# When a kernel loads its weight blocks, and when it begins to sum them: one transformer trunk on one NeuronCore

## The chip, the core and the metric

The kernel runs on one core of a Trainium2 chip, as one program. The metric is the device time of that program in microseconds (us); the median of the runs counts. The core has a matrix engine (TensorE, PE in the profile, with its weight loads as PEld), a vector engine (VectorE, DVE), a scalar engine (ScalarE, ACT), GpSimd (POOL) and SyncE (SP). SP and POOL issue the DMA transfers that this text is about; all transfers of the core run on the same 16 DMA engines.

## The reference

One residual stream of 512 tokens by 1024 features passes a short gated convolution layer, a feed-forward layer, a sliding-window attention layer with sinks, and a second feed-forward layer, each with a norm before and after it. The change touches the two feed-forward layers:

```python
D_MODEL = 1024; SEQ = 512; DEPTH = 2; D_FF = 2816
def swiglu(h, w_gate_up, w_down):
    g, u = jnp.split(h @ w_gate_up, 2, axis=-1)
    return (jax.nn.silu(g) * u) @ w_down
...
    ff = swiglu(rmsnorm(h, ffn_pre_norm[l]), ffn_w_gate_up[l], ffn_w_down[l])
    h = h + rmsnorm(ff, ffn_post_norm[l])
```

All data are float32. The kernel keeps that precision by splitting every operand into a high and a low part of a reduced float type and adding three matmuls for each product (high times low, high times high, low times high).

## The kernel before

**Products of 2x2 blocks.** Most large matrix products are done by blocks with seven products instead of eight (P1 to P7). For that, some products need weight blocks that are sums of others. The kernel makes these sums in DRAM while it runs: POOL issues DMAs that copy a block of 512 KB into a tile `hsum` and DMAs that add another block onto it. A copy is one kind of transfer here, an accumulate the other.

**Stages of a feed-forward layer.** The 22 feature tiles are taken as follows. Two go first, without the block scheme (`project_first`). The other 20 make ten pairs, called q0 to q9 here; each is a list of seven jobs, P1, P2, P6, P5, P7, P3, P4 (`gate_jobs`). Between them stand four lists of jobs for the down projection, d0 to d3 (`down_jobs`): d0 has 11 jobs, the others seven. The order is q0 q1 q2 d0 q3 q4 d1 q5 q6 d2 q7 q8 q9 d3. The last four weight blocks of the layer stand among q9 and d3 as jobs of their own.

**The line of jobs.** `in_line` (L474) walks through these jobs. Weight blocks arrive in seven buffers of 512 KB (`N_RAW = 7`, pool `wraw`), loaded by SP at L440, tile `raw`. For job j, `prepare(j)` splits its block: ACT writes the high part `whi` (L469), DVE the low part `wlo` (L470). This runs three jobs ahead of TensorE (`LINE_LEAD = 3`). After that DVE's read, the buffer is free, and `prepare` lets further loads be written into the program. A load waits on SP for the release of the buffer it takes. DVE adds two blocks in place (L457) where a product's sum is not made in DRAM: in pairs with a number in `ADDED` (1, 2, 3, 4, 5 and 7) only two sums are made in DRAM, `ab` and `ac`. There, block a11 is read by jobs P1, P6 and P3, and a12 by P2 and P3, so these two buffers are held longer than the ones loaded after them.

**The sums' plan.** `BEGIN` (L29) names, for each point of the program, the sum whose making begins there: `g07` is layer 0, pair q7; `d02` is layer 0, down list d2. Points: `0f0` and `0f1` lie in and behind `project_first` of layer 0, `0p3` at the end of q3, `0s1` at the end of d1. At each point `sum_on` (L558) first issues what is left, then gives the next step of each sum that is under way. A sum begins with its copies (two, or four where four tensors are made), goes on with two accumulates, and where four tensors are made, with one more and one more: two or four steps, one a point. The DMAs of a step go to a list, and behind each job `issue` (L529) takes `1 + len(issues) // 6` of them, each held back until ACT has made the high part of the block of job j + 3, so that they are paced.

The rule for loads, as it stands, is this one line (L488): the load with number n may be written when the block loaded seven before it has had its last use.

Of the kernel before, what the change touches and what calls it, by code (L numbers as in the profile page):

```python
# [27 lines left out]

BEGIN = {  # L29
# [4 lines left out]
}  # L34


# [18 lines left out]
N_SLOT, N_WIDE, N_RAW, N_W = 43, 14, 7, 4  # L55
# [17 lines left out]
def yoco_kernel(  # L73
# [400 lines left out]
    def in_line(jobs, late, paced=True):  # L474

        raws = []
        for j, job in enumerate(jobs):
            for raw in job.raws:
                if raw not in raws:
                    raws.append(raw)  # L480
                raw.last = j
        n = [0]

        def prepare(j):

            if 0 <= j < len(jobs):
                jobs[j].prepare()
            while n[0] < len(raws) and (n[0] < N_RAW or raws[n[0] - N_RAW].last <= j):  # L488
                raws[n[0]].fetch()
                n[0] += 1  # L490
            if j + 1 < len(jobs):
                jobs[j + 1].add()

        for j in range(-1, LINE_LEAD):
            prepare(j)
        late = late()
        for j, job in enumerate(jobs):
            if job.run:
                job.run(job)
            prepare(j + LINE_LEAD)  # L500
            if paced and j + LINE_LEAD < len(jobs):
                issue(1 + len(issues) // 6, jobs[j + LINE_LEAD].begun)
            for _ in range(1 if paced else max(len(late) - 1, 1)):
                if late and not job.alone:
                    late.pop(0)()
            late += job.then() or [] if job.then else []
# [22 lines left out]
    def issue(n, behind=None):  # L529

        for dst, src, op in issues[:n]:
            if len(dst.shape) == 3:
                dst, src = (t.rearrange("k (a b) c -> (k a) (b c)", b=4) for t in (dst, src))
            else:
                dst, src = (t.rearrange("(a b) c -> a (b c)", b=2) for t in (dst, src))
            kw = {} if op is None else {"accum_op": op}
            made = tc.keep_in_program_order(
                nc.gpsimd.dma_start(dst, src, max_dma_last_dim=4 * 4 * S, **kw))  # L538
            if behind is not None:
                tc.add_manual_dep(  # L540
                    made.ins, behind.ins.name, mybir.DependencyInfo(
                        mybir.DependencyClass.Sync, mybir.DependencyReason.DATA),
                    reason="pace")
        del issues[:n]
# [115 lines left out]
    with tc.manual_schedule(engines=ALL):  # L660
# [25 lines left out]
        for k in range(KT):  # L686
# [7 lines left out]
            for i in range(3):  # L694
                for t in range(3):
                    n = 3 * k + t
# [117 lines left out]
    with tc.manual_schedule(engines=ALL):  # L814
        project(begun[1][2], ws[2], xs)

        def late():
            parts = []
            for f in range(2):
                first, second, taps, third, end = conv(f)  # L820
                first(begun[f][0])
                second(begun[f][1])
                parts += [taps, lambda third=third, f=f: third(begun[f][2])]
                sum_on(f"c{f}")
                issue(len(issues))
            return parts + end()
# [645 lines left out]
    with tc.manual_schedule(engines=ALL):  # L1472
        sum_on("a0")
        for i in range(KT + 2):
# [6 lines left out]
            for c in ORDER.split():  # L1481
# [9 lines left out]
                op, n = c[0], [int(d) for d in c[1:].rstrip("-")]  # L1491
                t = i - late
                if op == "g":

                    u = 2 * (t - EARLY - 1) + n[0]
                    if u in (-2, -1, 2, 3):
                        j = u + 2 if u < 0 else u
# [8 lines left out]
                elif op == "G":  # L1506
                    t += LEAD + 1
                    of = qs
                    if KT <= t < KT + 4:
                        j = t - KT  # L1510
# [107 lines left out]
```

## Time and profile before

| | |
|---|---|
| median of 3 runs | 1024.08 us (1023.93 to 1025.08) |
| the profiled execution, its own time | 1026.6 us |
| span in that profile, first to last instruction | 1024.8 us |
| TensorE clock granted in it | 0.998 of full speed |
| TensorE busy | 1013.6 us, 99% |
| DVE, ACT, POOL busy | 857.8, 580.7, 196.7 us |
| feed-forward layer 0, q0 to the first job of d3 | 204.25 to 472.04 us |
| feed-forward layer 1, the same | 709.65 to 976.42 us |

The profile comes from one execution, 2.5 us above the median; 1.8 us of its own time lie outside the span. Times inside it are us from the span's start. A row of the timeline gives start, length, engine, line, operation and tiles; equal neighbours are merged with their count, and in brackets stands what ended the idle time before it. A row of the stretches gives the length of a stretch, busy time and count of each engine, the granted clock, the mean busy share of the 16 DMA engines, and GB/s. Layer 1's stages lie 505.4 us behind those of layer 0 up to d2 (709.65 less 204.25).

### The profile page before, as it was taken

To read this page: it belongs to the slowest core of one execution; us is meant where nothing else is said; L and a number is where in the kernel's file an instruction comes from. 1 tells how busy PE (TensorE), PEld (TensorE's weight loads), DVE (VectorE), ACT (ScalarE), POOL (GpSimd) and SP (SyncE) were. 2 spreads that over 40 slices of the span, in tenths; PEclk is the share of its full clock that TensorE was granted. 3 is DMA by queue.
4 is the path that set the end of the run, shared out by engine and by line. 5 is a ranking of instruction groups with operands and counts; after the bars stand their busy time and mean duration, and the time that the engine had idled before them with its cause. 6 is when DMAs were issued, how large, how long until landed. Compare 5 with 4: busy or idle time off the path is not lost.

```text
span 1024.8 us, 16537 instructions
## 1 busy us (share of the span) xinstructions
PE 1013.6 (99%) x6168; PEld 901.8 (88%) x6168; DVE 857.8 (84%) x1440; ACT 580.7 (57%) x1035; POOL 196.7 (19%) x259
## 2 busy tenths in 40 slices
PE   9999999999999999999999999999999999999997
PEld 8888888999899898898898888889998998989986
DVE  5766768889789988988869998778997898889896
ACT  7222445875655454566476776667666554645641
POOL 0443033112111111000122653232111010100001
PEclk9999999999999999999999999999999999999999
DMA  9897789459979699778504889976899576998742
GB/s 356 287 255 232 187 254 348 140 169 281 344 249 299 195 302 318 256 215 303 182 1 152 199 234 281 246 260 156 262 289 333 169 247 228 299 294 245 242 150 82
DMA packets 66576, 244.52 MB, mean 239 GB/s; under 512 B 7872, under 2 KB 8384, under 8 KB 54720
## 3 DMA queue, kind: packets, MB, share of 16 engines
q1 hardware_dynamic: 51328, 145.98, 38.9%
q0 software_dynamic: 14592, 96.48, 37.2%
q8 instruction: 48, 0.79, 0.3%
q10 hardware_dynamic: 576, 1.02, 0.3%
q14 instruction: 32, 0.26, 0.1%
HBM read 237.15 MB, written 102.76 MB: 332 GB/s over the span
## 4 chain that ended last, share of the span: by engine, by line
PE 80%; DVE 11%; DMA 4%; ACT 2%; issue 2%; POOL 0%; DVEq 0%; ACTq 0%
PE gx L1047 10%; PE gx L1050 5%; DMA raw<-in_w_gb_dram 4%; PE pcub L193 4%; PE pcub L191 4%; PE pcub L192 4%; PE gz L193 3%; PE gz L192 3%; PE gz L191 3%; PE px L191 3%; PE px L192 3%; PE px L193 3%; PE pmix L192 2%; PE pmix L191 2%; PE pmix L193 2%
## 5 line engine op out<-in xcount | busy, mean ns | idle before, releaser
L470 DVE TENSOR_TENSOR wlo<-raw,whi 128x1024 fp32r<-128x1024 f32 x225 | 274.6, 1227 | 65.6 <-ACT whi L469 65.6
L469 ACT ACTIVATE whi<-raw 128x1024 fp32r<-128x1024 f32 x225 | 233.8, 1051 | 108.3 <-DVE raw L457 25.0
L1047 PE MATMUL gx<-xt,whi 128*128 128x512 f32 x480 | 120.4, 393 | 0.7 <-DVE st L1008 0.7
L1047 PEld LDWEIGHTS gx<-xt,whi 128*128 128x128 f32 x480 | 86.3, 189 | 16.6 <-DVE st L1008 1.2
L538 POOL DMA_DIRECT2D hsum<-in_w_gb_dram x96 | 63.4, 747 | 141.4 <-ACT whi L469 82.3
L1024 ACT ACTIVATE st<-gx 128x256 f32<-128x256 f32 x120 | 42.7, 379 | 60.8 <-PE gx L1050 36.4
L538 POOL DMA_DIRECT2D hsum<-hsum x32 | 25.2, 789 | 260.1 <-ACT whi L469 208.2
L1050 PEld LDWEIGHTS gx<-xt,wlo 128*128 128x128 f32 x480 | 65.5, 190 | 4.7
L1050 PE MATMUL gx<-xt,wlo 128*128 128x256 f32 x480 | 66.9, 282 | 0.0
L1008 DVE TENSOR_TENSOR st<-gx,st 128x256 f32<-128x256 f32 x160 | 62.8, 420 | 3.4 <-ACT st L1024 1.6
L192 PE MATMUL pcub<-xhi,whi 128*128 128x512 f32 x168 | 65.4, 389 | 0.0
L191 PE MATMUL pcub<-xlo,whi 128*128 128x512 f32 x168 | 65.4, 389 | 0.0
L193 PE MATMUL pcub<-xhi,wlo 128*128 128x512 f32 x168 | 65.4, 389 | 0.0
L1063 ACT ACTIVATE gr<-gr 128x1024 f32<-128x1024 f32 x20 | 21.3, 1063 | 50.6 <-DVE gr L1008 50.6
L191 PE MATMUL px<-wlo,ahi 128*128 128x512 f32 x120 | 46.8, 390 | 0.1
L192 PE MATMUL px<-whi,ahi 128*128 128x512 f32 x120 | 46.7, 389 | 0.0
L193 PE MATMUL px<-whi,alo 128*128 128x512 f32 x120 | 46.7, 389 | 0.0
L193 PE MATMUL gx<-xhi,wlo 128*128 128x256 f32 x160 | 45.4, 284 | 0.8 <-DVE wlo L470 0.8
L193 PE MATMUL gz<-xhi,wlo 128*128 128x256 f32 x160 | 45.5, 284 | 0.0
L191 PE MATMUL gx<-xlo,whi 128*128 128x256 f32 x160 | 45.4, 283 | 0.0
L191 PE MATMUL gy<-xlo,whi 128*128 128x256 f32 x160 | 45.3, 283 | 0.0
L192 PE MATMUL gy<-xhi,whi 128*128 128x256 f32 x160 | 45.3, 283 | 0.0
(265 smaller groups left out, 3062.8 us busy)
## 6 DMA issues: line engine op xcount, KB each, us to landing
hsum<-in_w_gb_dram POOLq DMA_DIRECT2D x96, 512.0 KB, 7.8
raw<-hsum SPq DMA_DIRECT2D x88, 512.0 KB, 7.9
raw<-in_w_gb_dram SPq DMA_DIRECT2D x60, 512.0 KB, 7.7
hsum<-in_w_dn_dram POOLq DMA_DIRECT2D x36, 512.0 KB, 9.1
raw<-in_w_dn_dram SPq DMA_DIRECT2D x32, 512.0 KB, 6.1
hsum<-hsum POOLq DMA_DIRECT2D x28, 512.0 KB, 6.7
raw<-in_w_in_dram SPq DMA_DIRECT2D x21, 512.0 KB, 8.1
hsum<-in_w_dn_dram POOLq DMA_DIRECT2D x12, 768.0 KB, 12.2
```

What stands on the lines that cost most here:

```text
L191: nc.tensor.matmul(out, whi, xlo, start=start, stop=False, **kw)
L192: nc.tensor.matmul(out, whi, xhi, start=False, stop=False, **kw)
L193: nc.tensor.matmul(out, wlo, xhi, start=False, stop=stop, **kw)
L469: self.begun = nc.scalar.activation(hi[:, :n], raw, AF.Copy)
L470: nc.vector.tensor_tensor(out=lo[:, :n], in0=raw, in1=hi[:, :n].bitcast(F32), op=ALU.subtract)
L538: nc.gpsimd.dma_start(dst, src, max_dma_last_dim=4 * 4 * S, **kw))
L1008: nc.vector.tensor_tensor(out=out, in0=a, in1=b, op=ALU.add)
L1024: nc.scalar.activation(ste, a, AF.Copy)
L1047: nc.tensor.matmul(banks[c][e], whi[:, kk], factors[p][k][2], start=opened and k == 0, stop=False, **kw)
L1050: nc.tensor.matmul(banks[c][e][:, :256], wlo[:, kk], factors[p][k][0], start=False, stop=k == 3 and p == 4, **kw)
L1063: nc.scalar.activation(kept[2], kept[2], AF.Silu)
```

## The change

Two things are edited. The rule for loads no longer looks at the block seven before: it counts the blocks already loaded whose last use is still to come, and loads while these are fewer than seven. And in the plan, sums begin at earlier points. In layer 0, g05, g06, d02, g07 and g09 begin one point sooner, and g08 two points sooner (d0 lies between). In layer 1, g17 and g19 begin one point sooner and g18 two. The number of sums, of DMAs and of loads is the same, and no compute instruction is added or taken away.

```diff
 BEGIN = {
     "c0": "g00", "c1": "g01", "c3": "g02", "c4": "d00", "c6": "g03", "o0": "g04", "o1": "d01",
-    "0f1": "g05", "0p0": "g06", "0p1": "d02", "0p2": "g07", "0p3": "g08", "0s1": "g09", "0p5": "d03",
+    "0f0": "g05", "0f1": "g06", "0p0": "d02", "0p1": "g07", "0p2": "g08", "0p4": "g09", "0p5": "d03",
     "a0": "g10", "a1": "g11", "a3": "g12", "a4": "d10", "a6": "g13", "a7": "g14", "a8": "d11",
-    "1f0": "g15", "1f1": "g16", "1p0": "d12", "1p2": "g17", "1p3": "g18", "1s1": "g19", "1p5": "d13",
+    "1f0": "g15", "1f1": "g16", "1p0": "d12", "1p1": "g17", "1p2": "g18", "1p4": "g19", "1p5": "d13",
 }
...
-            while n[0] < len(raws) and (n[0] < N_RAW or raws[n[0] - N_RAW].last <= j):
+            while n[0] < len(raws) and sum(raw.last > j for raw in raws[:n[0]]) < N_RAW:
                 raws[n[0]].fetch()
                 n[0] += 1
```

## The prediction

> **What bounds the kernel now.** I read the page's busy times first, then TensorE's own waits, then the stretches stage by stage, then the chain of work where TensorE had waited.
>
> ```profile
> span 1024.8 us, 16537 instructions
> PE 1013.6 (99%) x6168; PEld 901.8 (88%) x6168; DVE 857.8 (84%) x1440; ACT 580.7 (57%) x1035; POOL 196.7 (19%) x259
> q1 hardware_dynamic: 51328, 145.98, 38.9%
> q0 software_dynamic: 14592, 96.48, 37.2%
> ```
>
> TensorE is idle for 11.2 us of 1024.8. No transfer or sum that only overlaps with it can cost time, so all that this change can save lies where TensorE waits for a weight block. Its waits in the two feed-forward layers are these, in all:
>
> ```profile
> PE gx L193 <- DVE wlo L470: 0.8, 1, 0.8
> PE gx L1047 <- DVE st L1008: 0.7, 2, 0.5
> ```
>
> Both hang on the split blocks. The stretches place them (length, PE, PEld, DVE, ACT, POOL, clock, DMA share, GB/s). The rows are q0, d0, q6, d2 and q7 of layer 0, then d0 and q7 of layer 1:
>
> ```profile
> 204.25:224.10 19.85, 19.85 (x146) 18.84 (x145) 17.22 (x27) 14.19 (x22) 1.83 (x3) 1.00 0.63 212
> 263.95:292.53 28.58, 28.58 (x128) 23.65 (x127) 21.57 (x30) 16.79 (x24) 3.41 (x5) 1.00 1.00 344
> 371.30:391.19 19.89, 19.89 (x147) 18.88 (x146) 17.34 (x28) 12.22 (x20) 4.47 (x7) 1.00 0.91 253
> 391.19:410.35 19.16, 19.16 (x86) 15.59 (x85) 14.51 (x22) 6.83 (x9) 2.36 (x3) 1.00 1.02 323
> 410.35:430.20 19.85, 18.82 (x134) 17.56 (x134) 19.47 (x28) 11.47 (x17) 1.56 (x2) 1.00 0.76 246
> 769.35:797.93 28.58, 28.58 (x128) 23.65 (x127) 21.57 (x30) 16.67 (x24) 2.61 (x4) 1.00 0.88 293
> 915.65:935.60 19.95, 19.48 (x140) 18.25 (x139) 18.18 (x27) 11.59 (x18) 1.55 (x2) 1.00 0.80 259
> ```
>
> Only q7 is hurt, in both layers, and it follows stretches in which the DMA engines were full (1.02). The chain of waits names the transfer (start, length, what), and PE's timeline shows the first gap:
>
> ```profile
> 389.06 20.07 DMA raw<-in_w_gb_dram
> 423.33 2.11 PE gx L1047 x8
> 429.28 1.84 PE gx L1047 x8
> 896.80 19.04 DMA raw<-in_w_gb_dram
> 927.71 2.11 PE gx L1047 x8
> ```
> ```profile
> 410.57 0.28 PE L192 MATMUL gx<-xhi,whi 128*128 128x256 f32 x1
> 411.61 0.39 PE L193 MATMUL gx<-xhi,wlo 128*128 128x256 f32 x1 [0.76 <-DVE wlo L470]
> ```
>
> A block of q7 took 20 us to land. **The ceiling of the gain** follows. Idle time in q7 is 19.85 - 18.82 = 1.03 us in layer 0 and 19.95 - 19.48 = 0.47 in layer 1. Behind a wait a group of eight matmuls takes 2.11 us instead of 1.84, once in each layer: 0.54. That makes 2.04. The first gap is larger by starts than by idle time (411.61 - 410.57, less the 0.12 us between neighbours as in the rows at 292.53 below, is 0.92, not 0.76), and its neighbours start slowly too, so up to 2.4. I take 2.2 us.
>
> **The rule for loads costs and gains nothing.** By the old rule, the load of q2's sum `ab` is written into the program only behind the split of job P3 of q1, two splits later than the buffer it takes is freed by that of P5. Yet SP issued it, with the next one, as follows (DVE's two splits are those of P6 and P5):
>
> ```profile
> 230.36 2.39 SPq L440 DMA_DIRECT2D raw<-hsum  x2
> 227.98 2.35 DVE L470 TENSOR_TENSOR wlo<-raw,whi 128x1024 fp32r<-128x1024 f32 x2
> ```
>
> It went at 230.36, 0.03 us behind the DVE read that ended at 227.98 + 2.35 = 230.33. SP waits for the buffer, not for a place in the program, and SP's queue holds the loads in the same order under either rule. So no load should start earlier. If I am wrong, loads in q1 to q5 and q7 would go out up to two jobs (two sevenths of a pair's 19.89, 5.7 us) earlier into a queue with spare room; since only q7 waits, that is worth nothing beyond the ceiling, and its cost is bounded by the same collisions as below.
>
> **What one transfer costs.** From the DMA queues' shares in three stretches: 324 to 334.5 us (only copies on q0), 334 to 352 (only two accumulates), 376 to 410 (both):
>
> ```profile
> q0 software_dynamic: 245, 1.57, 36.0%
> q1 hardware_dynamic: 1303, 2.75, 67.5%
> q0 software_dynamic: 160, 1.05, 33.0%
> q0 software_dynamic: 800, 5.24, 61.4%
> q1 hardware_dynamic: 1864, 4.49, 36.6%
> ```
>
> 1.57 MB are three blocks of 0.524 MB: 0.360 x 10.5 / 3 = 1.26 us of all 16 engines for a copy. Loads in that stretch: 0.675 x 10.5 / (2.75 / 0.524) = 1.35 us a block. An accumulate is 0.33 x 18 / 2 = 2.97 us. The third stretch holds six accumulates and four copies, 0.614 x 34 = 20.9 us, and with copies at 1.26 an accumulate is 2.64. I take 1.26, 1.4 and 2.65.
>
> **Where the sums go.** Stepping the plan through by hand gives the DMAs on POOL's queue in each stage (accumulates + copies), layer 0, before and after: behind `project_first` 2+0 and 2+2; q0 1+2 and 3+4; q1 3+4 both; q2 2+4 and 3+2; d0 3+2 and 4+4; q3 4+0 and 3+0; q4 1+4 and 1+0; d1 2+0 and 1+4; q5 1+4 and 2+0; q6 3+4 and 1+4; d2 3+0 both; q7 2+0 and 1+0. The counts before agree with the rows (POOL x7 in q6, x5 in d0). Layer 1 differs before the change in q2 (3+0) and d0 (2+2), and becomes like layer 0 from q2 on.
>
> In q6 this takes away two accumulates, 5.3 us of DMA time, and q5 before it is lighter by 1.26 x 4 - 2.65 = 2.4. The block that took 20.07 us stood behind q6's seven sums, of which these are the first and the last:
>
> ```profile
> 376.00 0.80 POOL L538 DMA_DIRECT2D hsum<-hsum  x1 [9.17 <-ACT a L580]
> 387.69 0.50 POOL L538 DMA_DIRECT2D hsum<-in_w_dn_dram  x1 [0.97 <-ACT whi L469]
> ```
>
> With 5.3 us less ahead of it, it lands at about 409.1 - 5.3 = 403.8 or sooner; its matmuls start at 410.35, and split takes 2.3 us. So q7's waits go: **-2.2 us**. Bounds: -2.4 and -1.0 (if only the direct wait goes).
>
> POOL itself issues more DMAs in `project_first` and d0, 0.5 to 0.8 us each; behind them in its queue stand only further sums, so that is free. The extra 2+2 of q0 are 7.8 us, against 0.37 x 19.85 = 7.3 us of idle DMA time there, and what spills into q1 is 0.5 us.
>
> **What is late next: d0.** It is full already (1.00 in layer 0), and gets one more accumulate and two more copies: 2.65 + 2.52 = 5.2 us, q2 another 0.1. The block next in line is that of q3's P1:
>
> ```profile
> 270.16 5.33 SPq L440 DMA_DIRECT2D raw<-in_w_gb_dram  x2
> DMA to landing us min/median/max: 15.7/15.7/15.7
> 286.01 1.06 ACT L469 ACTIVATE whi<-raw 128x1024 fp32r<-128x1024 f32 x1 [2.16 <-DVE s L585]
> 289.26 1.22 DVE L470 TENSOR_TENSOR wlo<-raw,whi 128x1024 fp32r<-128x1024 f32 x1
> 292.53 0.28 PE L191 MATMUL gx<-xlo,whi 128*128 128x256 f32 x1
> 292.77 0.28 PE L193 MATMUL gx<-xhi,wlo 128*128 128x256 f32 x1
> 775.56 0.33 SPq L440 DMA_DIRECT2D raw<-in_w_gb_dram  x1
> DMA to landing us min/median/max: 9.4/9.4/9.4
> 267.89 1.45 SPq L440 DMA_DIRECT2D raw<-hsum  x2
> DMA to landing us min/median/max: 11.3/11.3/11.3
> 291.17 0.39 PE L191 MATMUL px<-wlo,ahi 128*128 128x512 f32 x1
> ```
>
> Each row of landing times belongs to the SP row above it (the first load of it): q3's P1 in layer 0, the same in layer 1, and, for the rivals, the load of d0's last but one job.
>
> q3's block lands at 270.16 + 15.7 = 285.9. The first matmul that reads `wlo` starts at 292.77, and ACT and DVE need 1.06 + 1.22 + 0.1, so a landing up to 290.4 costs nothing. With all 5.3 us ahead of it, it lands at 291.2: **+0.8 us** in layer 0. If the two queues shared the engines evenly, half of it, 288.5: nothing. If it suffers as the block at 389.06 did, the whole wait of q7 moves here: +1.3. In layer 1 the same block lands at 785.0, in layer 0's time 279.6; d0 gets 2+2 more (7.8 us) and q2 two copies (2.5), less the idle DMA time of d0, 0.12 x 28.58 = 3.4: 279.6 + 4.4 to 279.6 + 10.3, at most 289.9. **0**, bounds 0 and +0.7.
>
> By the two rows of DMA queues at the top, a packet of q0 takes 0.372 x 1024.8 x 16 / 14592 = 0.42 us, one of q1 0.389 x 1024.8 x 16 / 51328 = 0.12. The Trainium skill, "DMA: Bandwidth & Descriptors", section "Queues, rings and completion order", says that each DMA engine takes turns between its queues a packet at a time; by that rule waiting sums get 77% of the time and the 5.3 us fall nearly all on the loads, and by an even split of time the sum would be 0.8 us lower. The trace speaks for the rule: from 376 to 410 sums had 61.4% against 36.6%.
>
> **The sum**: -2.2 + 0.8 + 0 = -1.4 us; on the profiled execution's own 1026.6 (span 1024.8, 1.8 outside it, 2.5 above the median) it gives 1025.2, on the median of 1024.08 it gives 1022.7.
>
> **Rivals.** Full gain: q7's waits go and d0 stays within its slack (loads get in between the sums). For it: 4.5 us of slack at that block, layer 1 unhurt. Against it: d0's DMA share is 1.00. -2.2 to -2.4: 1021.8 us.
>
> The wait moves: what q7 loses, q3 gets (1.3 + 0.7 to 0.9). For it: d0 will have eight sums, and seven stood before the late block of q7. Against: DVE has more room there (21.57 of 28.58 us). About 1024.1 us.
>
> Slower: ACT takes blocks in order, and a late block of d0's own last jobs (its load leaves at 267.89) holds it and all that it evacuates behind it. At 20.07 us that block lands at 288.0, is split at 290.3, and is needed when d0's last but one job starts: the last job's six matmuls take 292.53 - 291.17 = 1.36 us, the twelve before them twice that, so at 288.45. That is 1.8 us, and then q7's pattern behind it (1.3), in both layers 6.2, less 2.2: 1028.1 us. It decides if that load takes over 18.3 us, where it takes 11.3 now: 7 us more, with 5.3 us more work in front.
>
> **How the numbers follow.** Chances: forecast 0.42, full gain 0.26, moved 0.20, slower 0.12. 0.2% of this time, about what a measurement tells from no change, is 2.05 us: faster by more takes most of the full-gain case, 0.25; slower by more is the last rival, 0.12; the rest, 0.63, lies within. The range runs from 1021.5 (the ceiling, 1021.7, less the scatter of the median) to 1025.3 (the wait moved, with its bounds), and leaves out the slower rival and a part of the others.
>
> **What would show it.** Right: the load of q7's P1 in both layers lands within 10 us, q7's PE idle time falls under 0.2 us, loads still leave 0.02 to 0.03 us behind a DVE read, DMA share in q6 falls and in q0 and d1 rises, and the load issued at 270.16 lands near 291 with a new gap under 1 us at q3's start. Wrong: loads of q1 to q5 leaving earlier; no gap at q3; a gap of over 1.5 us there, or one inside d0; q7 still waiting.

## The result, and the profile after

The changed kernel takes 1031.47 us (median of 10 runs, 1026.43 to 1033.94), the kernel before 1024.23 us (1023.62 to 1026.02) on the same chip: a ratio of 1.0061, with a 95% interval of 1.0047 to 1.0074. It is slower by 5 to 8 us. The prediction, 1022.7 us with a range to 1025.3, was wrong.

The profiled execution of the changed kernel took 1033.94 us, the slowest of the ten, so the sizes below lie at the upper end. From its page come the span, the engines' busy times, and the two DMA queues; then TensorE's waits (us in all, times, the longest):

```profile
span 1032.1 us, 16533 instructions
PE 1015.8 (98%) x6168; PEld 903.1 (87%) x6168; DVE 857.8 (83%) x1440; ACT 582.4 (56%) x1035; POOL 197.3 (19%) x259
q1 hardware_dynamic: 51328, 145.98, 39.1%
q0 software_dynamic: 14592, 96.48, 36.6%
```
```profile
PE px L191 <- DVE mix L639: 6.5, 2, 4.3
```

The work is the same: packets, bytes and DVE's 857.8 us haven't moved. The two waits on `wlo` (L470) and `st` (L1008) are gone from the list, and a wait that the kernel before did not have stands in their place: TensorE waits until DVE has read a `px` bank into `mix`. The stretches say where (same columns as before; the rows are q0, d0, q6, d2 and q7 of layer 0, then d0 and q7 of layer 1):

```profile
203.81:223.66 19.85, 19.85 (x146) 18.85 (x145) 17.21 (x27) 14.21 (x22) 4.49 (x7) 1.00 0.73 203
263.51:296.17 32.66, 30.48 (x129) 24.71 (x127) 22.31 (x31) 16.92 (x24) 5.27 (x8) 0.95 1.02 344
374.93:394.82 19.89, 19.89 (x147) 18.89 (x145) 17.34 (x28) 12.23 (x20) 2.83 (x5) 1.00 0.85 285
394.82:413.89 19.07, 19.07 (x87) 15.77 (x85) 18.82 (x26) 7.92 (x10) 2.38 (x3) 1.00 0.97 295
413.89:433.74 19.85, 19.85 (x145) 18.85 (x144) 17.14 (x26) 11.62 (x17) 0.77 (x1) 1.00 0.58 174
771.23:805.97 34.74, 30.44 (x129) 24.74 (x128) 22.26 (x31) 16.69 (x24) 5.25 (x8) 0.95 0.97 326
923.69:943.60 19.91, 19.91 (x146) 18.91 (x145) 17.20 (x26) 11.69 (x17) 0.77 (x1) 1.00 0.56 171
```

Both q7 rows have no idle time left. Both d0 rows have grown: 32.66 - 28.58 = 4.1 us in layer 0 and 34.74 - 28.58 = 6.2 us in layer 1, together 10.2. Less the 2.0 to 2.4 us of q7's waits that makes 7.8 to 8.2; the span grew by 7.3, so 0.5 to 0.9 us are not placed. POOL's x8 in both d0 rows are the 4+4 DMAs, for x5 and x4 before.

The chain of waits through d0 of layer 0 (start, length, what) names every link but gaps of 0.1 us and less:

```profile
268.59 18.98 DMA raw<-hsum
287.68 0.64 ACT whi L469
288.34 0.69 DVE wlo L470
289.03 0.33 DVE s L584
289.37 0.34 DVE s L585
289.70 0.61 DVE mix L639
290.36 0.50 PE px L191
```

The load is that of d0's last job. DVE works through its queue in order, as these rows show, and in that queue the split of this block stands ahead of the `mix` that reads the two `px` banks. The job that runs next on TensorE adds its products into those very banks. So TensorE stood still, not for the block that was late, whose matmuls come one job later still, but for a bank that was read only behind its split. The first two matmuls after the waits, from PE's timeline, and the clock in the microseconds after them, from stretches of their own:

```profile
290.36 0.50 PE L191 MATMUL px<-wlo,ahi 128*128 128x512 f32 x1 [2.18 <-DVE mix L639]
800.20 0.80 PE L191 MATMUL px<-wlo,ahi 128*128 128x512 f32 x1 [4.30 <-DVE mix L639]
```
```profile
291.40:294.70 3.30, 3.30 (x10) 2.52 (x8) 3.30 (x5) 1.99 (x3) 0.00 (x0) 0.52 1.02 412
801.00:803.00 2.00, 2.00 (x6) 1.54 (x6) 2.00 (x4) 0.57 (x2) 0.00 (x0) 0.50 1.04 424
```

Behind each wait the granted clock was about half for some 3 us. In layer 0 the idle time is 2.2 us of the 4.1; the rest is the slow clock.

How late the load came is read from SP's rows for it and their landing times: kernel before, then the changed one, in layer 1 (in layer 0 it took 13.3 before, issued at 269.03, and 18.98 in the chain above):

```profile
L440 SPq DMA_DIRECT2D raw<-hsum x1: 320/320/320, 774.4 to 774.4; - x1
DMA to landing us min/median/max: 8.4/8.4/8.4
```
```profile
L440 SPq DMA_DIRECT2D raw<-hsum x1: 319/319/319, 776.3 to 776.3; - x1
DMA to landing us min/median/max: 19.4/19.4/19.4
```

In layer 1 the chain runs through another block, that of d0's last job but one, whose split stands one place further ahead in the same queue:

```profile
775.18 19.88 DMA raw<-hsum
796.25 1.23 DVE wlo L470
798.19 0.27 DVE wlo L470
799.54 0.61 DVE mix L639
800.20 0.80 PE px L191
```

The first `wlo` is the split of this block, the second that of the last one, which had landed by then. So either of the two blocks can hold back the `mix`. Some 1.7 of the 4.3 us TensorE would have waited in any case, as the split of the block that its next job reads ended only at 797.48.

### The profile page after: what moved, and what is told of

Same layout as the page of the kernel before. It is cut to its first block, busy times and chain, and to the rows that moved or that the text cites. A ratio compares the mean times of both kernels' runs of the same rounds, so it can differ in the third digit from the quotient of the medians.

```text
span 1032.1 us, 16533 instructions
## 1 busy us (share of the span) xinstructions
PE 1015.8 (98%) x6168; PEld 903.1 (87%) x6168; DVE 857.8 (83%) x1440; ACT 582.4 (56%) x1035; POOL 197.3 (19%) x259
## 4 chain that ended last, share of the span: by engine, by line
PE 77%; DVE 12%; DMA 6%; ACT 2%; issue 2%; POOL 0%; DVEq 0%; ACTq 0%
PE gx L1047 9%; DMA raw<-hsum 6%; PE gx L1050 4%; PE pcub L191 4%; PE pcub L193 4%; PE pcub L192 4%; PE gz L193 3%; PE gz L192 3%; PE gz L191 3%; PE px L191 3%; PE px L193 3%; PE px L192 3%; PE pmix L192 2%; PE pmix L191 2%; PE pmix L193 2%
## 5 line engine op out<-in xcount | busy, mean ns | idle before, releaser
L470 DVE TENSOR_TENSOR wlo<-raw,whi 128x1024 fp32r<-128x1024 f32 x225 | 274.7, 1227 | 74.4 <-ACT whi L469 74.3
L1047 PEld LDWEIGHTS gx<-xt,whi 128*128 128x128 f32 x480 | 86.3, 189 | 15.4
L1008 DVE TENSOR_TENSOR st<-gx,st 128x256 f32<-128x256 f32 x160 | 62.7, 420 | 3.4 <-ACT st L1024 1.6
L193 PE MATMUL gy<-xhi,wlo 128*128 128x256 f32 x160 | 45.3, 283 | 0.0
## 6 DMA issues: line engine op xcount, KB each, us to landing
hsum<-in_w_dn_dram POOLq DMA_DIRECT2D x12, 768.0 KB, 12.7
```

The costliest lines, as they stand in the source:

```text
L193: nc.tensor.matmul(out, wlo, xhi, start=False, stop=stop, **kw)
L470: nc.vector.tensor_tensor(out=lo[:, :n], in0=raw, in1=hi[:, :n].bitcast(F32), op=ALU.subtract)
L1008: nc.vector.tensor_tensor(out=out, in0=a, in1=b, op=ALU.add)
L1047: nc.tensor.matmul(banks[c][e], whi[:, kk], factors[p][k][2], start=opened and k == 0, stop=False, **kw)
```

## Experiments

The theory after this reading: the sums that the plan puts into d0 delay the loads of its last blocks, DVE's queue carries the delay to a `mix`, and the rule for loads plays no part. Medians below stand beside 1024.5 to 1024.8 us of the kernel before in the same sessions.

**The rule alone** (the plan as before):

```diff
-            while n[0] < len(raws) and (n[0] < N_RAW or raws[n[0] - N_RAW].last <= j):
+            while n[0] < len(raws) and sum(raw.last > j for raw in raws[:n[0]]) < N_RAW:
```

> The kernel before with the new rule for loads alone. Theory (the rule moves no load, since SP waits for the release of a buffer and not for a place in the program; the plan does all): 1024.2 us, as before, with q7's first gap of 0.8 us still there and the load of the block that ended late in d0 taking about 13 us. Rival (loads written sooner crowd d0's own): part of the 7 us, 1026 or more, with a gap inside d0.

Measured: 1024.43 us, ratio 1.0003 (0.9994 to 1.0012). The rule does nothing. What missed is the gap: q7 of layer 0 showed none, and the load of q7's P1 took 15.3 us for the 20.1 of the first profile; the load in d0 took 15.5 where about 13 was expected.

**The plan alone** (the rule as before, the plan as changed):

> The new points of the plan alone, with the old rule for loads. Theory: all of the slowdown, about 1031 us, with TensorE waiting on DVE's mix inside d0 in both layers (2 to 4.5 us each) and no gap in q7. Rival (the rule is what hurts, or half of it): 1022 to 1027 us.

Measured: 1030.69 us, ratio 1.0064 (1.0047 to 1.0080), with waits on `mix` of 1.37 and 2.65 us in the two d0's, the first under the 2 that were expected. The whole slowdown is the plan's.

**The kernel before, once more:**

> The kernel before, unchanged, for a second profile of it. If the q7 wait of the first profile is in every execution, it shows a gap of about 0.9 us at q7's start in layer 0 and a load of 20 us ahead of it; if that profile, 2.5 us above the median, held a rare one, this one has a load of 15 to 18 us there and no gap, and lies at 1023.6 to 1024.6 us.

Measured: 1024.18 us, q7's P1 loaded in 17.6 us, and no wait. The q7 rows of layer 0 of this profile and of the rule alone:

```profile
410.19:430.04 19.85, 19.85 (x144) 18.81 (x143) 18.76 (x28) 12.01 (x18) 1.56 (x2) 1.00 0.83 266
```
```profile
410.05:429.90 19.85, 19.85 (x145) 18.84 (x144) 19.02 (x27) 11.80 (x18) 1.56 (x2) 1.00 0.86 277
```

TensorE is busy for all of 19.85 us in both. The waits that the prediction took away were in one of three profiles, the one 2.5 us above the median. The span of this one is 1022.4 us, 2.4 shorter than the first.

**g08 and g18 begun behind d0** (all else as changed):

```diff
-    ... "0p2": "g08", ...
+    ... "0s0": "g08", ...
-    ... "1p2": "g18", ...
+    ... "1s0": "g18", ...
```

> The changed kernel, but g08 and g18 begin behind d0 and not ahead of it, so that their four copies leave d0 (4+4 DMAs become 4+0; by 1.26 us a copy, 5.0 us of DMA time, about what the change had put in) and q3 gets 1+4. Theory (sums queued in d0 delay the load of d0's last block): that load falls from 19 us to about 13 or 14, no wait on mix in d0, and q7's gaps stay away since q6 keeps its 1+4: 1021.8 to 1022.5 us. Rival (d0 is hurt by the accumulates, 4 for 3, or by what q2 leaves over): the wait stays, 1027 or more.

Measured: 1024.04 us, ratio 0.9998 (0.9989 to 1.0006). The load of d0's last block took 11.2 us in layer 0 and 15.5 in layer 1, and neither d0 nor q7 waits (d0 of layer 0, d0 and q7 of layer 1):

```profile
263.43:292.01 28.58, 28.58 (x128) 23.65 (x127) 21.58 (x30) 16.67 (x24) 3.13 (x4) 1.00 0.99 318
767.01:795.60 28.59, 28.59 (x129) 23.66 (x127) 21.67 (x30) 16.67 (x24) 3.13 (x4) 1.00 1.00 325
913.32:933.20 19.88, 19.88 (x145) 18.87 (x144) 17.18 (x26) 11.64 (x17) 0.78 (x1) 1.00 0.57 172
```

In each layer, g08 or g18 begun one point later, which takes four copies out of d0, turns the slowdown into no difference. The time expected, 1021.8 to 1022.5, was missed: with every wait in the feed-forward layers gone, the kernel is not measurably faster than before. This is the best version that these experiments lead to; it beats the changed kernel, not the one before.

**The split moved behind the mix.** The DMAs are those of the changed kernel; only the split of d0's last block, and the load written with it, come one job later. For that one job, the sums are held back until ACT has split the block before, not this one (the edit of `issue` that does so is left out here):

```diff
-            prepare(j + LINE_LEAD)
+            k = j + LINE_LEAD
+            held = [k < len(jobs) and jobs[k].held, k - 1 < len(jobs) and jobs[k - 1].held]
+            if held[1]:
+                prepare(k - 1)
+            if not held[0]:
+                prepare(k)
...
+            jobs[-1].held = len(cs) > 1
```

> The changed kernel with the same DMAs, but the split of d0's last block (ACT's whi, DVE's wlo) and the load written behind it come one job later in the program, behind the mix that empties px. Theory (TensorE waits for a mix that stands on DVE behind that late split, not for the weights): in layer 0 the wait falls from 2.3 us to under 0.6, as the block is needed only at 291; in layer 1 there remains the wait for the block before it, which landed at 795.06 and is split at 797.4, where TensorE stood from 795.7: about 1.8 us; in all 1031.5 less 4 to 7, 1024.5 to 1027.5 us. Rival (TensorE waits for the weight block itself, so that order on DVE doesn't matter): no change, 1031 us.

Measured: 1026.60 us, ratio 1.0030 (1.0015 to 1.0044). The load still took 17.7 us in layer 0, over the 16.6 that it may take ahead of that `mix` (worked out below). DVE's timeline there shows `mix` ahead of the short split, and PE's the job that had waited:

```profile
287.73 1.28 DVE L644 TENSOR_TENSOR mix<-mix,px 128x512 f32<-128x512 f32 x2
288.92 1.27 DVE L644 TENSOR_TENSOR mix<-mix,py 128x512 f32<-128x512 f32 x2
290.12 0.68 DVE L470 TENSOR_TENSOR wlo<-raw,whi 128x512 fp32r<-128x512 f32 x1
```
```profile
288.62 0.40 PE L191 MATMUL px<-wlo,ahi 128*128 128x512 f32 x1
```

No bracket: the matmul waited for nothing, though by that limit the block was 1.1 us late. In the changed kernel, too, the block that this job reads was split by 285.85 + 1.23 = 287.08, 3.3 us before TensorE went on. That rules out a wait for the weights themselves in layer 0 and shows the order on DVE as the link. Some 2 to 3 us over the kernel before remain, and four of the twelve runs took 1029.7 to 1032.3 us. This profile, of a run of 1025.41 us, doesn't show what those runs waited for, and the wait of about 1.8 us expected in layer 1 is not in it. That the rest comes from the block of the job before, which landed late in layer 1 too, is argued, not shown.

**One layer at a time** (the old points in the other):

> The changed kernel with the old points in layer 1. Theory (each layer's d0 pays by itself): a wait on mix in layer 0 alone, 0 to 2.5 us by the execution and 1.7 more where the clock falls behind it, and none in layer 1, where the load of d0's last block takes 8 to 9 us: 1026.5 to 1028.5 us. Rival (layer 1 carries it all, as it got 4+4 for 2+2 where layer 0 had 3+2 already): 1024.0 to 1025 us.

> The changed kernel with the old points in layer 0. Theory (each layer pays, and a sum's DMA time ahead of a load delays it in full): the load of d0's last block in layer 1 takes 18 to 20 us for 8.4, a wait on mix in layer 1 alone, 1027 to 1029 us; the two layers' excess over before adds up to the 6 to 7 us of the whole change. Rival (idle DMA time in layer 1's d0 takes up half, as the prediction had it): a load of 13 to 15 us, no wait, 1024 to 1025 us.

Measured: layer 0 alone 1025.71 us, ratio 1.0012 (1.0003 to 1.0022); layer 1 alone 1029.28 us, ratio 1.0037 (1.0024 to 1.0050). The waits, each the only one of its kind in its profile:

```profile
289.78 0.50 PE L191 MATMUL px<-wlo,ahi 128*128 128x512 f32 x1 [1.59 <-DVE mix L639]
```
```profile
795.74 0.80 PE L191 MATMUL px<-wlo,ahi 128*128 128x512 f32 x1 [3.54 <-DVE mix L639]
```

Both layers pay, layer 1 about three times as much, where the load of the last block took 20.3 us. The time of layer 0 alone lies under the 1026.5 to 1028.5 us that were expected, that of layer 1 just over its range. The two excesses add up to 0.49% for 0.61% of the whole change, the same within the intervals.

**Half the dose in layer 0** (the kernel before, with g07 and g08, g17 and g18 exchanged):

> The kernel before with g07 and g08 (g17 and g18) changing places in the plan: in layer 0, d0 gets 3+4 DMAs where it had 3+2, half of what the change adds there. Theory (each us of sums put ahead of a load in d0 delays it by one us): the load of d0's last block, 13.3 us before, takes 15.8, still within the 16.6 that DVE's queue leaves it, so no wait on mix, and 1024.0 to 1024.6 us. Rival (any copies of g08 in d0 stall it): a wait in layer 0 and 1026 or more.

Measured: 1024.66 us, ratio 0.9996 (0.9986 to 1.0005). The time is about as expected, the load isn't: in the profiled execution, the slowest of the ten at 1026.17 us, it took 17.2 us and TensorE waited 2.11. The chain behind this wait runs through the block of the last job but one, which took 17.7 us. Four profiles with the old plan in layer 0 (the first, the rule alone, the one taken once more, layer 1 alone) have the load of the last block at 13.3, 15.5, 14.2 and 12.7 us. Loads this close to their limits (worked out below) pass them in some executions.

**One DMA a job:**

```diff
-                issue(1 + len(issues) // 6, jobs[j + LINE_LEAD].begun)
+                issue(1, jobs[j + LINE_LEAD].begun)
```

> The changed kernel with one DMA a job from the list of sums, in place of 1 + a sixth of the list: d0 has the same 4+4, but its eight DMAs are spread over eight jobs and two or three of the copies leave only when the late block has landed. Theory (only what is queued before a load lands delays it): 2.5 to 3.8 us less ahead of it, so it takes 15 to 16.5 us, the waits on mix shrink to under 1 us, and the time falls to 1024 to 1026.5 us, unless what is left over at the ends of other stages makes a wait there. Rival (what counts is the DMA work of the whole stage): 1030 us or more.

Measured: 1025.08 us, ratio 1.0011 (1.0001 to 1.0020); the load took 16.7 us in layer 0 and 13.8 in layer 1, with no wait on `mix` in this profile, of a run of 1024.88 us. Three of the twelve runs took 1028.0 to 1029.1 us, so something is left in some executions. The stage has the same eight DMAs, so what counts is mostly what is queued ahead of the load, not the stage's total.

**Smaller packets for the sums:**

```diff
-max_dma_last_dim=4 * 4 * S
+max_dma_last_dim=2 * 4 * S
```

> The changed kernel with the rows of the sums' DMAs cut from 8 KB to 4 KB, so that a packet of a sum takes about half the 0.42 us; bytes, DMAs and order are the same. Theory (the 16 engines take turns packet by packet, so that sums get more of them than loads): loads in d0 get more turns, the load of the last block falls from 19 to 15 to 17 us, the waits on mix mostly go, 1025 to 1028 us. Rival (the queues share by time or by bytes, or the loads' delay is the sums' whole work in any case): no change, 1030 to 1031.5 us.

Measured: 1025.72 us, ratio 1.0015 (1.0004 to 1.0026). From its page, the sums' queue, and from PE's timeline the one wait on `mix` left:

```profile
q0 software_dynamic: 26368, 96.48, 37.8%
```
```profile
795.83 0.50 PE L191 MATMUL px<-wlo,ahi 128*128 128x512 f32 x1 [2.00 <-DVE mix L639]
```

A packet took 0.378 x 1026.3 x 16 / 26368 = 0.235 us for 0.42, with bytes and order untouched, and the excess over the kernel before fell from 0.61% to 0.15%, by 4.7 us. The load took 14.9 us in layer 0 but 18.3 in layer 1, hardly less than the 19.4 with large packets; this profile is of a run of 1028.08 us, 2.4 above the median, and the chain behind its wait runs through the block of the last job but one, which took 17.6 us for 19.88. So the time speaks for turns by the packet, against a share by time or bytes; layer 1's row does not, and how far the rule carries there stays open.

## Why the prediction was wrong

**The rule: right.** In the changed kernel too, SP issues the load that the prediction looked at 0.03 us behind DVE's second split (229.93 for 227.55 + 2.35):

```profile
229.93 0.33 SPq L440 DMA_DIRECT2D raw<-hsum  x1
```
```profile
227.55 2.35 DVE L470 TENSOR_TENSOR wlo<-raw,whi 128x1024 fp32r<-128x1024 f32 x2
```

**q7's waits: mechanism right, size wrong.** The waits went, and the block that took 20.07 us took 6.5. That is 13.6 us less, where the prediction's own sum has 5.3 for the two accumulates; the rest of it no run here takes apart. But the sum took 2.2 us off the median, and the median hardly held them. The prediction noted that the profiled execution was 2.5 us above the median and did not ask whether these 2.4 us of waits were that difference. They very likely were: two other profiles of the same queues have none, the one of the unchanged kernel with a span 2.4 us shorter, and the version without any wait gains 0.02% (0.11% to a loss of 0.06%).

**"What is late next: d0": the step that failed.** Its sign of being wrong, a gap inside d0, is what came. It took q3's P1 to be "the block next in line". That block did land at 290.12, near the 291.2 worked out for it. But the one in front, d0's last, had less room, and its room is set by DVE's queue. In the chain above, TensorE starts 290.36 - 287.57 = 2.79 us after the landing (268.59 + 18.98). In the kernel before, d0's last but one job starts at 288.45, so the limit for that landing was 285.66, 16.6 us after the issue at 269.03. It took 13.3. There were 3.3 us of room for 5.3 us of added sums: 2.0 us late, where 2.2 were measured. In the profiles with one layer changed and with the plan alone, loads of 18.4, 20.3, 18.2 and 19.5 us are 1.8, 3.7, 1.6 and 2.9 over this limit, and TensorE waited 1.59, 3.54, 1.37 and 2.65.

**Layer 1: a term put at 0 that was 6.2.** The step "less the idle DMA time of d0" failed. (The list of stages also left out that layer 1 differs before the change in q0, q1, q3 and q4; nothing here rests on it.) Sums of 7.8 + 2.5 = 10.3 us were added, and the load went from 8.4 to 19.4 us, by 11.0. The idle DMA time did not help, as it lay behind this load: in the kernel before, the DMA share was 0.99 while the load was under way and 0.73 from its landing to the end of d0:

```profile
774.41:782.80 8.39, 8.39 (x39) 6.95 (x38) 4.62 (x4) 5.35 (x7) 1.11 (x3) 1.00 0.99 278
782.80:797.93 15.13, 15.13 (x68) 12.53 (x67) 11.93 (x19) 7.67 (x11) 0.00 (x0) 1.00 0.73 277
```

With 10.3 us on the load, the same limit gives 8.4 + 10.3 - 16.6 = 2.1 us of waiting. In the profile it was more, 4.3 us, since the block before was the one that held the queue. From its landing at 795.06 to the matmul at 800.20 it took 5.14 us, which puts its own limit at 288.45 - 5.14 - 267.89 = 15.4 us. It took 8.8 us before, and 8.8 + 10.3 - 15.4 = 3.7.

**The slower rival: right place, wrong link.** It had a late block of d0's own last jobs holding an engine that takes things in order, and its block, that of the last job but one, is the one in layer 1's chain; in layer 0 it is the last. The rival put the queue on ACT instead of DVE, and let the load take 18.3 us, as it looked only at the block's own use; with the `mix` behind it the limit is 15.4, and for the last block 3.3 us of delay were enough. Hence 0.12 for what happened. It also had no term for the clock: 1.7 us in layer 0 (4.1 less 2.34, the wait counted between the starts of matmuls) and about as much in layer 1, a third of the 10.2.

**The turns of the queues: borne out where they were used.** The prediction took the sums' 5.3 us to fall on the loads nearly in full. In the first two profiles they did, in both layers (5.7 for 5.3, 11.0 for 10.3). The other profiles of the two plans scatter, with 12.7 to 15.5 against 18.2 to 18.4 us in layer 0, and 7.5 to 8.3 against 19.5 to 20.3 in layer 1. With g08 begun behind d0, q2 and d0 get by the same prices 0.3 us more than in the kernel before in layer 0 and 5.3 more in layer 1, and the load moved by -2.1 and +7.1. So the sum is good to some 2.5 us, not better.

## What to carry to other kernels

A transfer's limit is not the moment its own consumer runs: follow the block through the in-order queue of the engine that unpacks it, and look what else stands behind it there, above all an operation that reads out an accumulator. Before a stall seen in a profile is taken off a median, ask whether that execution's distance from the median is the stall. And DMA work moved into a stage delayed the loads queued beside it by about its full time here, so room is to be measured at the tightest load, not as the stage's idle share.

## What was not expected of the hardware

Short idle times can halve TensorE's clock here. After idle times of 2.18, 2.65, 3.54 and 4.30 us the granted clock fell to 0.50 to 0.52; after 1.37, 1.59, 2.00 and 2.11 us in the same place it did not. In layer 0 of the changed kernel it fell 1 us after the matmuls had begun again, and matmuls that start every 0.23 us started every 0.43 for 3.3 us. 2.11 and 2.18 are too close to tell a threshold from a matter of phase.

The Trainium skill, "TensorE: Matmul & The Clock Gate", section "Part 1: The HAM clock gate (the "warmup" mystery)", says that the clock is gated to half after at least one idle window of about 3.4 us, that it is full again after a busy one of that length, and that the window runs freely. The half clock agrees with the traces (0.50 to 0.52), and so does its length of some 3 us, though behind the wait of 3.54 us it was 5; that a whole window must be idle does not, as 2.18 us were enough.
